# A two-layer decoder: the stores of turned keys and queries take the main part and the rest of one head in one transfer

## The chip, the cores and the metric

The kernel runs on one core of a Trainium2 chip and computes the whole forward pass in one launch. Its engines work side by side, each through its own queue of instructions: TensorE (PE in the profile; PEld is its loading of weights), VectorE (DVE), ScalarE (ACT), GpSimd (POOL) and SyncE (SP). Transfers are issued by SP and by POOL. The metric is the device time of one execution in microseconds.

## The reference

A hybrid decoder trunk in float32: sequence S = 1024, model width 1024, 16 heads of 64 in 4 key/value groups, two layers.

```
layer A:  h = rmsnorm(x);  proj = h @ w_in     # queries, keys and values of three branches, gates
          o = g0 * compressed_attention + g1 * attention_on_top_8_selected_blocks + g2 * window_attention(256)
          x = x + o @ w_out;   x = x + swiglu(rmsnorm(x))
shared:   K, V of three dilation groups from rmsnorm(x) @ kv_w
layer B:  q = rmsnorm(x) @ w_q                 # own queries for each of the three dilation groups
          o = three dilated window attentions ((128,1), (512,4), (2048,16)) merged by their softmax denominators
          x = x + o @ w_out;   x = x + swiglu(rmsnorm(x))
out = rmsnorm(x)
```

A relative-position bias (32 buckets, 16 heads) is added to every attention logit.

## The kernel before

**Numbers in two parts.** Where the kernel needs more than one reduced-precision product gives, it splits a float32 array into a main part H and a rest L (`split`): ACT writes H = source (L179, or L183 with a scale), DVE writes L = source - H (L180 and L184). A product is then three matmuls (`mm3`, L229 to L231). Queries and keys are kept as both parts.

**Layer A's projections.** `proj_T` computes 128 columns of the projection for 512 tokens, turned, so that features lie on partitions: 128 features are two heads of 64. The product lies in one of six PSUM banks named `mm`. `evac_q` and `evac_k` split it into two tiles, `sth` (H) and `stl` (L), of 128 x 512, each with two buffers. `store_heads` (L405) writes them to the DRAM arrays `qS` (per head: 64 rows of H, then 64 rows of L, by 1024 tokens) and `kS` (branch, group, part, 64, 1024), with one DMA for each head b and part z, on POOL's queue: four of 64 x 512 (128 KB) for each eviction. `store_blockind` uses an `sth` buffer too. POOL's queue in this stretch also holds the stores of values (`vS`) and of parts of the output weights (`wS`), and near the end the masks of layer A's attention: `load_bias` has POOL cut a window mask `TW` (affine_select) and a row `C` from each bias tile `T`.

**Layer A's attention** works through units of a group and 128 query tokens. SP loads, from `qS`, `kS`, and others, queries `Q` and `QM`, keys `K` and `KF`, window keys `KW`, values `V` and `VW`, and bias tiles `T` (from `sA`). A unit's window keys are two `KW` tiles (`load_kw`): each takes 64 columns of compressed keys (`kc`, L717) and two DMAs of 64 rows from `kS` (L346 and L347, the upper and the lower half). TensorE multiplies them with the queries at L758, turns the weights at L353 (`pt`) and multiplies with the values at L390.

**Layer B's projections** run as 18 jobs (`project_B`), six for shared keys and values and twelve for queries. For each half a job, `rows_out.done` splits the result into `chunk`, a pair of rows of the array `xr`: a tile of 128 x 2 x 1024 whose first row is H and whose second is L. There are four such chunks, taken in turn. After the second half of the tokens four DMAs on POOL (L1585) write 64 x 1024 (256 KB) each to `qB` or `kBs`. The stores of the last job (`last_stores`) wait by an explicit dependency for a bias load of the attention that follows. POOL's queue there also holds a good part of the sums of the projections' fast matrix multiplication (L1190 to L1208).

**What sets the order.** The program is traced in the order in which it is written; a scheduler then orders the instructions of each engine by a simulated timeline and by the dependencies between tiles. A transfer counts on one of eight completion semaphores for its kind of queue, taken in turn, so each transfer of a queue also waits for the one eight places before it.

## Time and profile before

| | |
|---|---|
| Time, three executions | 2796.76, 2796.29, 2792.22 us; median 2796.29 us |
| The profiled execution | 2793.83 us, of which the span is 2792.1 us; mean granted TensorE clock 0.997 |
| Busy in the span | PE 2738.9 (98%), PEld 2218.9, DVE 2214.7 (79%), ACT 1426.8, POOL 1402.8 us (50%) |
| Transfers | 315.13 MB, of these 62.99 MB in 20464 packets of POOL's queue |
| Stores touched by the change | qS 64 and kS 32 of 128 KB, qB 96 and kBs 24 of 256 KB |

All rows come from one profiled execution. The span runs from the first to the last recorded event. Times in the trace are us from its start; "busy" is the time in which an engine had an instruction at work, and what follows a `<-` in a row is the instruction that ended a wait.

### The profile page before, as it was taken

The page shows a single profiled execution, that of the slowest core. Times are in us where ns is not written, and L with a number is a line of the kernel's source. Part 1 is how long each engine was busy: PE and PEld are TensorE (multiplying, and loading weights), DVE is VectorE, ACT ScalarE, POOL GpSimd, SP SyncE. Part 2 cuts the span into 40 slices and gives each one's busy share as a digit, 9 for nine tenths or more (in the row PEclk, how much of TensorE's full clock was granted, in tenths as well). Part 3 has the DMA queues.
Part 4 walks back from the last instruction along what each step waited for, and adds up shares of the span by engine and source line. Part 5 has one row for each costly group of instructions (what it writes and reads, how often), then busy time and mean ns, then how long its engine had stood idle before and what let it go on. Part 6 is the DMA issues. An engine that isn't in the chain of part 4 may idle for free.

```text
span 2792.1 us, 43025 instructions
## 1 busy us (share of the span) xinstructions
PE 2738.9 (98%) x14494; PEld 2218.9 (79%) x14494; DVE 2214.7 (79%) x4527; ACT 1426.8 (51%) x3171; POOL 1402.8 (50%) x1454
## 2 busy tenths in 40 slices
PE   9999999999999999999999999999999999999997
PEld 8988676776788888888778888777778888888886
DVE  5453888887889899989875677688898888888987
ACT  5531777775644343333454444577756433343434
POOL 3135655552465566565457787110014756655652
PEclk9999999999999999999999999999999999999999
DMA  8669443224122322232224555786341211112112
GB/s 237 218 196 298 133 128 105 68 62 159 35 76 69 83 65 68 62 77 62 84 80 116 167 156 159 242 257 187 114 174 44 74 58 57 49 57 61 54 42 83
DMA packets 292924, 315.13 MB, mean 113 GB/s; under 512 B 50428, under 2 KB 229677, under 8 KB 292704
## 3 DMA queue, kind: packets, MB, share of 16 engines
q1 hardware_dynamic: 272240, 249.40, 30.5%
q0 software_dynamic: 20464, 62.99, 7.4%
q8 instruction: 115, 1.88, 0.3%
q14 instruction: 105, 0.86, 0.1%
HBM read 243.96 MB, written 81.95 MB: 117 GB/s over the span
## 4 chain that ended last, share of the span: by engine, by line
PE 85%; DVE 6%; ACT 2%; issue 2%; DMA 2%; POOL 1%; SPq 1%; POOLq 0%; DVEq 0%; ACTq 0%
PE ux L1161 18%; PE uy L1161 15%; PE dx L993 8%; PE o L390 7%; PE pt L353 6%; PE dr L993 6%; PE dr L1161 4%; PE mm L230 3%; PE mm L229 3%; PE mm L231 3%; PE s L758 1%; DVE pl L954 1%; PE s L846 1%; PE s L1808 1%; PE s L845 1%
## 5 line engine op out<-in xcount | busy, mean ns | idle before, releaser
L954 DVE TENSOR_TENSOR pl<-oT,ph 128x512 fp32r<-128x512 f32 x340 | 340.2, 1018 | 72.3 <-PE dr L993 17.4
L953 ACT ACTIVATE ph<-oT 128x512 fp32r<-128x512 f32 x346 | 211.8, 628 | 215.6 <-PE ux L1161 53.3
L954 DVE TENSOR_TENSOR pl<-oTb,ph 128x512 fp32r<-128x512 f32 x232 | 214.7, 948 | 27.2 <-PE dr L993 17.4
L953 ACT ACTIVATE ph<-oTb 128x512 fp32r<-128x512 f32 x238 | 145.5, 628 | 168.7 <-PE ux L1161 53.4
L353 PE MATMUL pt<-ident,P 128*128 128x128 f32 x1536 | 228.0, 278 | 3.3 <-DVE pT L356 1.9
L742 POOL TENSOR_SCALAR P<-P,sm,gates 128x384 f32<-128x384 f32 (+7 forms) x256 | 183.2, 727 | 79.3 <-DVE sm L740 54.8
L353 PEld LDWEIGHTS pt<-ident,P 128*128 128x128 f32 x1536 | 172.9, 140 | 61.8 <-issue 43.0
L998 DVE TENSOR_TENSOR xrfx<-xrfx,dr 128x512 f32<-128x512 f32 x320 | 204.2, 679 | 17.8 <-PE dr L993 17.7
L1354 POOL TENSOR_TENSOR oT<-oT,gffn 128x512 f32<-128x512 f32 x92 | 118.9, 1303 | 196.0 <-DMA oT<-in_ffn_w_up_dram 127.7
L998 DVE TENSOR_TENSOR xrfx<-xrfx,dx 128x512 f32<-128x512 f32 x320 | 204.5, 678 | 2.2 <-PE dx L993 2.2
L738 ACT ACTIVATE P<-P,m 128x384 f32<-128x384 f32 (+7 forms) x256 | 171.1, 670 | 36.0 <-DVE m L851 14.9
L356 DVE COPY pT<-pt 128x512 f32<-128x512 f32 (+1 forms) x224 | 143.2, 648 | 44.5 <-PE pt L353 39.8
L1354 POOL TENSOR_TENSOR oTb<-oTb,gffn 128x512 f32<-128x512 f32 x92 | 111.8, 1226 | 130.8 <-DMA oTb<-in_ffn_w_up_dram 79.0
L356 ACT COPY pT<-pt 128x512 f32<-128x512 f32 x192 | 110.1, 578 | 103.8 <-PE pt L353 100.8
L390 PE MATMUL o<-pT,V 128*64 128x256 f32 x1200 | 160.7, 391 | 2.3 <-ACT pT L356 1.5
L1770 ACT ACTIVATE P<-P,st 128x384 f32<-128x384 f32 (+2 forms) x256 | 139.6, 548 | 32.3 <-DVE st L1765 30.4
L1765 DVE CUSTOM_DVE_ANT_0 P<-s,T 128x384 f32<-128x384 f32 (+2 forms) x256 | 112.9, 478 | 10.5 <-PE pt L353 3.0
L390 PEld LDWEIGHTS o<-pT,V 128*64 128x64 f32 x1200 | 73.6, 136 | 51.8 <-issue 9.9
L993 PE MATMUL dx<-ph 128*128 128x512 f32 x320 | 107.5, 390 | 0.8 <-ACT ph L953 0.8
L993 PE MATMUL dx<-ph,pl 128*128 128x512 f32 x320 | 107.0, 389 | 0.0
L847 DVE CUSTOM_DVE_ANT_0 P<-s,T 128x128 f32<-128x128 f32 (+3 forms) x192 | 99.5, 550 | 8.1 <-PE s L846 7.8
L230 PE MATMUL mm<-hL,wh 128*128 128x512 f32 (+1 forms) x272 | 102.6, 378 | 0.0
(623 smaller groups left out, 8040.3 us busy)
## 6 DMA issues: line engine op xcount, KB each, us to landing
qB<-xrfx POOLq DMA_DIRECT2D x96, 256.0 KB, 4.5
oT<-in_ffn_w_up_dram SPq DMA_DIRECT2D x92, 256.0 KB, 2.9
oTb<-in_ffn_w_up_dram SPq DMA_DIRECT2D x92, 256.0 KB, 2.9
Q<-qB SPq DMA_DIRECT2D x40, 512.0 KB, 6.9
wd<-in_ffn_w_down_dram SPq DMA_DIRECT2D x60, 256.0 KB, 2.6
oT<-in_b_w_q_dram SPq DMA_DIRECT2D x48, 256.0 KB, 5.6
K<-kBs SPq DMA_DIRECT2D x40, 256.0 KB, 7.5
wraw<-in_a_w_in_dram SPq DMA_DIRECT2D x18, 512.0 KB, 6.9
```

Source lines behind the costliest of these rows:

```text
L230: nc.tensor.matmul(ps, lh, rl, start=False, stop=False, skip_group_check=bool(shared))
L353: prev = nc.tensor.transpose(ps[:, i * 128:(i + 1) * 128], h, ident)
L356: copy(t[:, :w], ps[:, :w])
L390: mm = nc.tensor.matmul(po[64 * e:64 * e + 64, :256], v[e], t, start=first and lo == i == 0, stop=last and hi == nb and i == len(ops) - 1, ...
L738: nc.scalar.activation(P[:, e, :n], P[:, e, :n], AF.Exp, bias=mm[:, e:e + 1], scale=-1.0, accum_out=sm[:, e:e + 1])
L742: nc.gpsimd.tensor_scalar(P[:, e, :n], P[:, e, :n], sm[:, e:e + 1], gate(e), op0=OP.mult, op1=OP.mult)
L953: nc.scalar.activation(h, src, AF.Copy)
L954: self.last = (eng or nc.vector).tensor_sub(l, src, f32(h))
L993: nc.tensor.matmul(banks[t], part(a, t)[u], b[v], start=z == 0 and onX != 2, stop=z == 2, skip_group_check=True)
L998: nc.vector.tensor_add(xs, xs, banks[t])
L1161: mm = nc.tensor.matmul(b, x[:, i * 128:(i + 1) * 128], ys[i], start=first and (z, i) == (0, 0), stop=(z, i) == (2, 3), skip_group_check=True)
L1354: nc.gpsimd.tensor_mul(v, v, gains[:, k:k + 4].unsqueeze(2).to_broadcast([128, 4, 128]))
```

## The change

Both parts go into one tile and one store takes both parts of one head. In layer A, `two_parts` makes one tile `st` of 128 x 2 x 512 with two buffers, in place of `sth` and `stl`, and `store_heads` issues one DMA of 64 x 2 x 512 (256 KB) for each head. In layer B the chunk is already one tile; the four DMAs become two of 64 x 2 x 1024 (512 KB). The addresses in `qS`, `kS`, `qB` and `kBs` and the bytes stay the same. The stores fall from 96 to 48 in layer A and from 120 to 60 in layer B.

```diff
     def store_heads(dst, t, cols):
         for b in range(2):
-            for z in range(2):
-                nc.gpsimd.dma_start(dst(b, z)[:, cols], f32(t[z][b * 64:(b + 1) * 64]))
+            nc.gpsimd.dma_start(dst(b)[:, :, cols], f32(t[b * 64:(b + 1) * 64]))
+
+    def two_parts():
+        t = st.tile([128, 2, 512], F32R, name="st", bufs=2)
+        return t, (t[:, 0, :], t[:, 1, :])
...
         def evac_k(i, ch):
             def f(ps, tk):
-                t = [st.tile([128, 512], F32R, name=n, bufs=2) for n in ("sth", "stl")]
-                split(*t, ps)
-                store_heads(lambda b, z: kS[i, 2 * ch + b, z], t, tk)
+                t, hl = two_parts()
+                split(*hl, ps)
+                store_heads(lambda b: kS[i, 2 * ch + b].rearrange("z d s -> d z s"), t, tk)
...
-                t = st.tile([128, 512], F32R, name="sth", bufs=2)
-                nc.scalar.copy(t[:16], raw)
-                nc.gpsimd.dma_start(bS[:, cols], f32(t[:16]))
+                t = two_parts()[0][:16, 0, :]
+                nc.scalar.copy(t, raw)
+                nc.gpsimd.dma_start(bS[:, cols], f32(t))
...
         def evac_q(ch):
             def f(ps, tk):
-                t = [st.tile([128, 512], F32R, name=n, bufs=2) for n in ("sth", "stl")]
-                split(*t, ps, -DH ** -0.5)
-                store_heads(lambda b, z: qS[2 * ch + b, z * 64:(z + 1) * 64], t, tk)
+                t, hl = two_parts()
+                split(*hl, ps, -DH ** -0.5)
+                store_heads(lambda b: qS[2 * ch + b].rearrange("(z d) s -> d z s", d=DH), t, tk)
...
-                    out[a] = t[:, 0, :].bitcast(F32R), t[:, 1, :].bitcast(F32R)
+                    out[a] = t[:, 0, :].bitcast(F32R), t[:, 1, :].bitcast(F32R), t
...
                     for b in range(2):
-                        for z in range(2):
-                            dst = qB[i, 4 * g + 2 * a + b, z * 64:(z + 1) * 64] if kind == "q" else \
-                                kBs[i, 2 * a + b, z]
-                            store = nc.gpsimd.dma_start(dst, f32(t[z][b * 64:(b + 1) * 64]))
-                            if n == len(jobs) - 1:
-                                last_stores.append(store)
+                        dst = qB[i, 4 * g + 2 * a + b].rearrange("(z d) s -> d z s", d=DH) if kind == "q" else \
+                            kBs[i, 2 * a + b].rearrange("z d s -> d z s")
+                        store = nc.gpsimd.dma_start(dst, t[2][b * 64:(b + 1) * 64])
+                        if n == len(jobs) - 1:
+                            last_stores.append(store)
```

The scheduler orders the changed program anew. The lines below give each engine's order at the places of interest; the numbers behind names tell tiles apart and differ between the two programs, and the changed program's lines lie three further down (two behind `rows_out`).

POOL near the end of layer A's projections, before: mask work for attention stands between the stores of main part and rest.

```order
L689 AFFINE_SELECT TW_2538<-T_2536 128x384
L692 COPY C_2535<-T_2536 128x32
L689 AFFINE_SELECT TW_2545<-T_2543 128x384
L692 COPY C_2535<-T_2543 128x32
L689 AFFINE_SELECT TW_2552<-T_2550 128x384
L692 COPY C_2535<-T_2550 128x32
L409 DMA qS<-sth 64x512 x2
L689 AFFINE_SELECT TW_2559<-T_2557 128x384
L692 COPY C_2535<-T_2557 128x32
L409 DMA qS<-stl 64x512 x2
```

And after:

```order
L408 DMA qS<-st 64x2x512 x6
L692 AFFINE_SELECT TW_2478<-T_2476 128x384
L695 COPY C_2475<-T_2476 128x32
L692 AFFINE_SELECT TW_2485<-T_2483 128x384
L695 COPY C_2475<-T_2483 128x32
L692 AFFINE_SELECT TW_2492<-T_2490 128x384
L695 COPY C_2475<-T_2490 128x32
L692 AFFINE_SELECT TW_2499<-T_2497 128x384
L695 COPY C_2475<-T_2497 128x32
L408 DMA qS<-st 64x2x512 x6
```

The mask work of the four heads is no longer parted by a store.

SP at the start of layer A's attention, before: the two window-key tiles of one unit (3164 and 3165), then the `force` and `QM` loads.

```order
L717 DMA KW_3164<-kc_90 128x64
L346 DMA KW_3164<-kS 64x384
L347 DMA KW_3164<-kS 64x384
L717 DMA KW_3165<-kc_91 128x64
L346 DMA KW_3165<-kS 64x384
L347 DMA KW_3165<-kS 64x384
L923 DMA force<-in_force_dram 128x128
L676 DMA QM_2880<-qS 64x4x512
```

After, the first two loads of the first tile (now 3092) are still ahead of `force` and `QM`; the rest stands behind four bias loads, five loads of keys and values, and four more bias loads, of which the last ones are:

```order
L704 DMA K_2933<-bS 16x1024
L725 DMA V_2938<-vS 128x4x64
L688 DMA T_3064<-sA 128x512
L688 DMA T_3071<-sA 128x512
L688 DMA T_3078<-sA 128x512
L688 DMA T_3085<-sA 128x512
L347 DMA KW_3092<-kS 64x384
L720 DMA KW_3093<-kc_91 128x64
L346 DMA KW_3093<-kS 64x384
L347 DMA KW_3093<-kS 64x384
```

So four loads of window keys moved behind fifteen other loads.

TensorE at the first use of these two tiles, before:

```order
L758 MATMUL s<-KW_3164,Q_2872 128x448
L758 MATMUL s<-KW_3165,Q_2872 128x448
L353 MATMUL pt<-ident,P_3119 128x128 x2
L758 MATMUL s<-KW_3164,Q_2874 128x448
L758 MATMUL s<-KW_3165,Q_2874 128x448
L845 MATMUL s<-K_2580,Q_2519 128x512
L846 MATMUL s<-KF_2586,Q_2519 128x512
```

And after:

```order
L353 MATMUL pt<-ident,P_2838 128x128
L353 MATMUL pt<-ident,P_2872 128x128
L761 MATMUL s<-KW_3092,Q_2800 128x448
L761 MATMUL s<-KW_3092,Q_2802 128x448
L848 MATMUL s<-K_2520,Q_2459 128x512
L849 MATMUL s<-KF_2526,Q_2459 128x512
L848 MATMUL s<-K_2520,Q_2461 128x512
L849 MATMUL s<-KF_2526,Q_2461 128x512
L353 MATMUL pt<-ident,P_2838 128x128
...
L761 MATMUL s<-KW_3093,Q_2800 128x448
L761 MATMUL s<-KW_3093,Q_2802 128x448
```

Both products with the first tile now come first, and those with the second after four products with `K` and `KF` and four transposes (`pt`). Six transposes more than before stand ahead of the first product: the two that stood between the products, and four of another unit's weights.

## The prediction

> **What bounds the kernel now.** I read the page's header and totals first, then the chain that ended last, then a table of stretches, and last the waits at the places that the change touches.
>
> ```profile
> span 2792.1 us, 43025 instructions
> ...
> PE 2738.9 (98%) x14494; PEld 2218.9 (79%) x14494; DVE 2214.7 (79%) x4527; ACT 1426.8 (51%) x3171; POOL 1402.8 (50%) x1454
> ...
> PE 85%; DVE 6%; ACT 2%; issue 2%; DMA 2%; POOL 1%; SPq 1%; POOLq 0%; DVEq 0%; ACTq 0%
> ```
>
> TensorE is busy for 98% of the span and carries 85% of the chain; POOL, which issues the stores, is half idle and has 1% of the chain. A saving on POOL counts only where TensorE is waiting for what comes behind POOL. The stores lie in two places: layer A's projections, in the second and third of the stretches below, and layer B's, mostly in the fourth. The stretches read: start and end, length, busy time of each engine (with instructions), the granted clock, DMA share, GB/s.
>
> ```profile
> 100.00:250.00 150.00, 150.00 (x776) 127.35 (x776) 72.44 (x101) 51.64 (x76) 45.97 (x87) 1.00 0.71 223
> 250.00:300.00 50.00, 47.64 (x236) 37.72 (x236) 23.20 (x131) 25.85 (x100) 32.40 (x70) 1.00 0.82 248
> ...
> 1450.00:1750.00 300.00, 298.25 (x1333) 245.92 (x1332) 206.60 (x206) 144.02 (x233) 231.17 (x252) 1.00 0.52 150
> 1750.00:1800.00 50.00, 48.12 (x295) 39.22 (x293) 27.04 (x62) 25.72 (x58) 4.19 (x8) 1.00 0.72 218
> ```
>
> In layer A's projections TensorE has no idle time at all (150.00 of 150). At the passage into attention it idles 2.36 us of 50, in layer B's projections 1.75 of 300, although POOL is 77% busy there, and 1.88 in the stretch behind them. That is 5.99 us in all: the most that anything near these stores could give.
>
> **The change, part by part.** First the issues. The groups show the number of instructions, their busy time and the mean of one in ns; the list of transfers shows the size and the median time from issue to landing.
>
> ```profile
> L1585 POOL DMA_DIRECT2D qB<-xrfx x96 | 51.0, 537 | 15.0 <-ACT xrfx L183 12.6 <-DMA T<-s 2.2
> ...
> L409 POOL DMA_DIRECT2D qS<-sth x32 | 17.1, 537 | 34.8 <-ACT sth L183 32.7 <-DMA wS<-ob 1.8 <-DMA qS<-stl 0.3
> ...
> L409 POOL DMA_DIRECT2D qS<-stl x32 | 16.9, 531 | 12.4 <-DVE stl L184 8.6 <-DMA wS<-ob 1.5 <-DVE bl L545 1.4
> ...
> L1585 POOL DMA_DIRECT2D kBs<-xrfx x24 | 12.8, 539 | 0.8 <-ACT xrfx L179 0.8
> ...
> L470 POOL DMA_DIRECT2D wS<-ob x16 | 9.0, 564 | 15.1 <-DVE ob L466 8.7 <-DVE ob L468 6.1 <-issue 0.3
> ...
> L409 POOL DMA_DIRECT2D kS<-sth x16 | 8.4, 532 | 23.3 <-ACT sth L179 23.3
> L409 POOL DMA_DIRECT2D kS<-stl x16 | 8.4, 529 | 6.4 <-DVE stl L180 6.3
> ```
>
> The stores are 216 issues: 17.1 + 16.9 + 8.4 + 8.4 + 51.0 + 12.8 = 114.6 us of POOL. After the change there are 108 with twice the bytes each. An issue of 128 KB costs 529 to 537 ns, one of 256 KB 537, one of 512 KB over 128 rows (wS) 564, so I take 0.53 to 0.56 us for a joined one: 108 make 57 to 60 us, and POOL is rid of 54 to 57 us. If a joined issue with its extra dimension cost two old ones, nothing would be freed.
>
> Who waited for these stores? The waits of ACT and DVE in layer A's projections and of TensorE in layer B's (total us, times, longest) say it.
>
> ```profile
> ACT sth L183 <- PE mm L231: 45.9, 11, 4.8
> ```
> ```profile
> DVE stl L184 <- DMA qS<-stl: 9.8, 2, 5.2
> ```
> ```profile
> PE ux L1161 <- ACT d L1210: 0.7, 1, 0.7
> PE dr L1161 <- DVE d L1236: 0.6, 1, 0.6
> ```
>
> In layer A the only ones held up were ACT and DVE when they wanted a store buffer back: DVE 9.8 us in two waits. ACT sits idle up to 4.8 us ahead of an eviction, waiting for TensorE's product, and TensorE has six banks to go on in; so none of it reached TensorE, whose idle time there is 0. In layer B what little TensorE waits is for ACT's and DVE's forming of differences (d), not for a store and not for POOL. So the 54 to 57 us are taken off a queue that nobody waits for. What they can give: in layer A 0; at the passage at most 0.5, since its waits are for DVE; in layer B's projections at most 0.5 of the 1.75. I take 0.6 in all, with 0 and the whole 5.99 as bounds.
>
> The Trainium skill's page "DMA: Bandwidth & Descriptors", section "Anatomy of one DMA — SWDGE (gpsimd) path", gives a transfer about 2.0 us of fixed cost and its bytes at 436 GB/s on top; by it 108 transfers fewer would take an estimated 216 us of fixed cost away, and the sum would go far down if those stood in line. No run so far shows them in line: TensorE's idle time in these stretches is 5.99 us.
>
> Second, the new wait. A row of DVE in layer A's projections shows how long it takes for a rest, and the list of transfers the landing of POOL's stores by size.
>
> ```profile
> 255.08 0.69 DVE L184 SCALAR_TENSOR_TENSOR stl<-mm,sth 128x512 fp32r<-128x512 f32 x1 [4.60 <-DMA qS<-stl]
> ```
> ```profile
> qB<-xrfx POOLq DMA_DIRECT2D x96, 256.0 KB, 4.5
> ...
> wS<-ob POOLq DMA_DIRECT2D x16, 512.0 KB, 5.1
> ```
>
> The main part, written by ACT, could leave while DVE was still forming the rest; the joined store waits for both, and both halves of a buffer come free together. One split on DVE is about 0.7 us, a joined transfer's landing lies by the sizes before between 4.5 and 5.1 us. So a buffer is held about 0.7 us longer at the main part. What is queued behind the waiting store on POOL is the next store and, at the passage, the mask work for attention; behind a late buffer stands ACT's next eviction, with its 4.8 us to spare. The wait that DVE had at the rest's buffer becomes ACT's. Cost 0; without that cover, 5.2 us a time at two places.
>
> Third, what the scheduler moved. Apart from the stores the orders of the engines are nearly the same, save at the start of attention A, where SP loads the window keys (KW, two tiles a unit, each of a kc row and two kS halves). Before, both tiles of one unit stand ahead of the force and QM loads; now the lower half of one tile and all of the other, four loads, stand behind those two, eight bias loads (T) and five of K and V. The lines show when SP issued them before, when TensorE used the keys first, and the landing times of that stretch.
>
> ```profile
> 286.97 0.60 SPq L346 DMA_DIRECT2D KW<-kS  x1
> 287.62 0.59 SPq L347 DMA_DIRECT2D KW<-kS  x1
> ...
> 290.19 0.58 SPq L923 DMA_DIRECT2D force<-in_force_dram  x1
> ...
> 297.54 5.46 SPq L685 DMA_DIRECT2D T<-sA  x4
> 304.05 0.50 SPq L717 DMA_DIRECT2D KW<-kc  x1
> ...
> 306.13 0.54 SPq L717 DMA_DIRECT2D KW<-kc  x1
> ```
> ```profile
> 302.01 0.66 PE L758 MATMUL s<-KW,Q 128*128 128x448 f32 x2
> 302.50 0.38 PE L353 MATMUL pt<-ident,P 128*128 128x128 f32 x2
> ...
> 303.12 0.39 PE L845 MATMUL s<-K,Q 128*128 128x512 f32 x1
> ...
> 304.03 1.04 PE L353 MATMUL pt<-ident,P 128*128 128x128 f32 x8
> 305.00 1.08 PE L390 MATMUL o<-pT,V 128*64 128x256 f32 x8
> ...
> 307.35 0.68 PE L758 MATMUL s<-KW,Q 128*128 128x448 f32 x2 [0.46 <-DVE cm L761]
> ```
> ```profile
> T<-sA SPq DMA_DIRECT2D x8, 256.0 KB, 5.4
> KW<-kS SPq DMA_DIRECT2D x13, 96.0 KB, 3.4
> K<-kS SPq DMA_DIRECT2D x3, 256.0 KB, 9.6
> ```
>
> Over the whole execution the loads of KW landed in:
>
> ```profile
> DMA to landing us min/median/max: 1.7/2.6/8.0
> ```
>
> The keys were issued 12 us ahead of use. Now TensorE's order puts six more transposes ahead of their first use (eight take 0.97 us, 304.03 to 305.00, so 0.7): about 302.74. The second tile comes after two more score products (0.49), four of K (0.91, 303.12 to 304.03) and four transposes (0.49): about 304.63. On SP the four loads leave 287.62 to 290.19 empty, so what stood behind moves 2.57 us ahead, and the late half is issued where SP was free again, at 304.05 - 2.57 = 301.48; with 3.4 us it lands at 304.88. The last of the other three follows 2.08 later (304.05 to 306.13), at 303.56, and lands at 306.96. TensorE would stand 304.88 - 302.74 = 2.14 us, and then be at the second tile at 304.63 + 2.14 = 306.77, 0.19 too early: 2.3 us in all. A K load of that stretch took 9.6 us; if the K loads don't come earlier, because the DMA engines and not SP limit them, the issue stays at 304.05 and the stand is 4.9. If landings are as fast as the shortest KW load, 1.7, the half is there at 303.18 and the second tile at 305.26, which costs 0.6. So 0.6 to 4.9, and I take 2.3, from SP's own rows. Of it I give 0.6 back: the 0.46 at 307.35 and one more wait for DVE of that size vanish when DVE has time to catch up. Net 1.7.
>
> A stand of that length may bring a second price. After 1.56 us of idle time at 2063.08 us, eight matmuls took 0.63 instead of 0.39 and the granted clock fell to half for some 2 us.
>
> ```profile
> 2063.08 0.50 PE L229 MATMUL dr<-ph 128*128 128x512 f32 x1 [1.56 <-DVE o L1859]
> ...
> 2064.03 0.63 PE L229 MATMUL dr<-ph 128*128 128x512 f32 x1
> ```
> ```profile
> 2064.00:2066.00 2.00, 2.00 (x6) 1.58 (x5) 2.00 (x3) 0.00 (x0) 0.76 (x1) 0.50 0.36 131
> ```
>
> Eight times 0.24 is 1.9 us, which I leave out of the sum, as idle time at 2060 came in several pieces, and take into the slow side. The Trainium skill's page "TensorE: Matmul & The Clock Gate", Part 1, lets the clock fall after an idle window of about 3.4 us: by it a stand of 2.3 would cost no clock and one of 4.9 would; the row at 2063 shows a fall after less.
>
> **The sum.** -0.6 (POOL) + 0 (the wait for both parts) + 1.7 (late keys) = +1.1 us. On the profiled execution (2793.83 us, its span 2792.1 and 1.7 around it) that is 2794.9. The median of the three executions is 2796.29, 2.5 above it, so the number to compare with other medians is 2796.29 + 1.1 = 2797.4. The executions themselves lie between 2792.22 and 2796.76, and 0.2% (5.6 us) is about what a measurement of this kernel can tell from no change.
>
> **Rivals.** Faster: the freed POOL time reaches TensorE, because the mask copies on POOL in the passage and the products ahead of layer B's differences come earlier. For it speaks POOL's 77% in layer B's projections; against it that no wait of TensorE there names POOL. Taking all 5.99 us of idle time in these stretches gives 2790.3; only with nearly all of it is the change measurable.
>
> Slower: the late window keys at 302 us. With 4.9 us of standing, 1.9 of lowered clock and nothing given back the time is 2796.29 - 0.6 + 6.8 = 2802.5. It decides when the late half lands after 307.0: the stand is then 4.3, with the clock 6.2, less 0.6 is 5.6. For it speaks the 9.6 us of the K loads and a longest KW landing of 8.0; against it that the scheduler also gave TensorE other work ahead.
>
> Nothing happens at all: the bytes and the rows of memory stay what they were, so the transfers keep the DMA engines as long as before, and the loads still land in time. That gives 2796; it lies within the same bound as my forecast.
>
> **How the numbers follow.** No measurable change, my forecast and the last rival together: 0.73. The faster rival 0.13, since it needs all idle time at once. The slower one 0.14, since its bound lies inside the landing times seen. The range goes from the faster rival's end, 2790, to the slower one's, 2803, and leaves out 1 to 2 in 10 for a mechanism that I don't see, or a set of executions at one edge of the spread.
>
> **What the trace after would show.** 48 and 60 stores at 0.53 to 0.56 us each on POOL, POOL's total near 1347 us; landing of a joined store near that of one before, or 0.5 longer; TensorE without idle time at 100 to 250 us; one or two waits of TensorE, 0.6 to 5 us together, at 302 to 307 us ahead of a score product with KW, its releaser a KW load; ACT now waiting for qS stores where DVE did. I'm wrong if joined stores take much longer to issue or land (then ACT's waits rise over 4.8 us and TensorE idles in layer A), or if the order in attention A moves more than this one stand.

## The result: 0.99% slower, and the time went in layer B's projections

Five executions of the changed kernel took 2820.04 to 2823.45 us, median 2821.61; five of the kernel before, on the same chip, 2789.37 to 2796.76, median 2796.29. The medians are 25.3 us apart; the ratio of the means is 1.0099 (95%: 1.0084 to 1.0113). The forecast was 2797.4 with a range to 2803.

The header, totals and chain by engine of the changed kernel's page:

```profile
span 2819.8 us, 42871 instructions
...
PE 2751.4 (98%) x14494; PEld 2223.7 (79%) x14494; DVE 2221.6 (79%) x4527; ACT 1423.0 (50%) x3171; POOL 1353.4 (48%) x1346
...
PE 78%; DVE 8%; DMA 5%; issue 3%; POOL 3%; ACT 2%; SPq 1%; POOLq 0%; DVEq 0%; ACTq 0%
```

POOL lost 49 us of work, and the program became longer by 28: TensorE's share of the chain fell from 85% to 78%, that of transfers rose from 2% to 5%, that of POOL from 1% to 3%. The same stretches as before (start and end, length, busy time of each engine, granted clock, DMA share, GB/s) say where:

```profile
100.00:250.00 150.00, 150.00 (x773) 127.17 (x773) 72.78 (x101) 51.70 (x76) 31.45 (x55) 1.00 0.70 224
250.00:300.00 50.00, 46.07 (x225) 37.45 (x225) 23.25 (x136) 26.64 (x105) 26.18 (x58) 0.97 0.84 244
1450.00:1750.00 300.00, 283.15 (x1235) 229.20 (x1233) 185.42 (x186) 129.33 (x214) 193.76 (x184) 0.98 0.49 136
1750.00:1800.00 50.00, 47.59 (x207) 38.80 (x208) 31.66 (x35) 21.22 (x34) 21.30 (x22) 1.00 0.62 177
```

Layer A's projections are untouched. In layer B's, TensorE gets through 1235 matmul records in 300 us where it got through 1333: 98 fewer at 0.224 us each (298.25 / 1333) is 22 us of work not done. Idle time explains 15.1 of it (298.25 - 283.15); the granted clock, 0.98 for 1.00, about 6 (2% of 300). Fixed places of the program agree: the kernel is 2.6 us late ahead of layer B's projections (1433.3 for 1430.7 us) and 26.9 late at their end (the last product with T1h 1790.9 for 1764.0). It is 32.6 late at the last write to xr, and 27.7 at the end of the span; where the 5.7 us between the projections and that write go, no run separates. What gives about 4.8 us back at the end is POOL's closing instruction, DRAIN, which is issued behind POOL's last work (before and after; of the three durations in ns, shortest, median and longest, the longest is the one meant):

```profile
L1961 POOLq DRAIN  x3: 46/98/11891, 2779.4 to 2791.8; - x3
```
```profile
L1963 POOLq DRAIN  x3: 46/98/4700, 2812.0 to 2819.6; - x3
```

Before, it ends 10.8 us after the last write to xr, when SP has been done for 4.8; after the change it ends 3.6 us after that write and SP, done at 6.0, is last. Its length goes with the number of transfers that POOL issues in the whole program: 11.9 us with 307 (before), 7.0 with 247 (b_only, b_128 and others below), 4.7 with 199 (after). Three runs are out of line, 2.7 in b_rows2k, 2.4 in b_pair and 2.9 in ab_pair, and why stays open. So the end hides about 4.8 us of loss, and the times below, of kernels with different numbers of stores, differ by this too.

What the engines wait for in layer B's projections, 1450 to 1750 us (total us, times, longest): first POOL before, then POOL, ACT and TensorE after.

```profile
POOL oT L1562 <- DMA oT<-in_b_w_q_dram: 27.6, 11, 5.1
```
```profile
POOL oT L1565 <- DMA oT<-in_b_w_q_dram: 54.6, 14, 9.0
```
```profile
ACT xrfx L183 <- DMA qB<-xrfx: 38.9, 7, 6.4
ACT ph L956 <- POOL oT L1206: 20.0, 6, 6.7
```
```profile
PE dr L1164 <- ACT ph L956: 10.9, 5, 2.7
PE ux L1164 <- ACT d L1213: 2.2, 1, 2.2
```

In the kernel before, ACT's wait for POOL's sums, the second of its two rows here, was shorter:

```profile
ACT ph L953 <- POOL oT L1203: 11.3, 5, 5.6
```

Two things are new after the change. POOL, which multiplies each query weight by its gain, waits for the weight load twice as long as before. And ACT waits 38.9 us for the joined stores themselves (before: 0), because it wants their buffer back. Behind ACT stands `ph`, the operand that TensorE waits for. ACT also waits longer for POOL's sums ahead of `ph`, 20.0 us for 11.3: a second way from POOL to TensorE, which does not go over the buffer. The list of transfers (size, median us to landing) and the groups on POOL show the stores:

```profile
qB<-xrfx POOLq DMA_DIRECT2D x48, 512.0 KB, 6.5
...
oT<-in_b_w_q_dram SPq DMA_DIRECT2D x48, 256.0 KB, 6.4
```
```profile
L1587 POOL DMA_DIRECT2D qB<-xrfx x48 | 29.0, 609 | 14.7 <-DVE xrfx L184 12.0 <-DMA T<-s 2.0 <-issue 0.7
...
L408 POOL DMA_DIRECT2D qS<-st x32 | 19.5, 612 | 63.0 <-DVE st L184 54.1 <-DVE bl L548 8.1 <-DVE dg L791 0.7
...
L408 POOL DMA_DIRECT2D kS<-st x16 | 9.7, 610 | 36.2 <-DVE st L180 36.2
...
L1587 POOL DMA_DIRECT2D kBs<-xrfx x12 | 7.3, 613 | 0.0
```

A joined store lands in 6.5 us (two stores of half the size: 4.5 each) and takes 609 to 613 ns to issue instead of 537.

One turn of the loop, from the timeline of POOL, ACT and TensorE, and from the chain in 1600 to 1650 us:

```profile
1608.59 1.22 POOL L1587 DMA_DIRECT2D qB<-xrfx  x2
1609.84 1.30 POOL L1208 TENSOR_TENSOR oT<-oT 128x512 f32<-128x512 f32 x1
1611.07 1.20 POOL L1587 DMA_DIRECT2D qB<-xrfx  x2
...
1621.55 1.04 POOL L1565 TENSOR_TENSOR oT<-oT,gmix 128x512 f32<-128x512 f32 x1 [6.00 <-DMA oT<-in_b_w_q_dram]
```
```profile
1620.76 1.12 ACT L183 ACTIVATE xrfx<-oT 128x512 fp32r<-128x512 f32 x1 [6.43 <-DMA qB<-xrfx]
...
1622.78 0.62 ACT L956 ACTIVATE ph<-oT 128x512 fp32r<-128x512 f32 x1
```
```profile
1619.91 1.07 PE L1164 MATMUL uy<-T2h,pl 128*128 128x512 f32 x4
1623.45 1.22 PE L1164 MATMUL dr<-B21h,ph 128*128 128x512 f32 x4 [2.47 <-ACT ph L956]
```
```profile
1612.14 9.25 DMA oT<-in_b_w_q_dram
...
1631.42 0.52 POOL qB L1587
1631.95 9.78 DMA qB<-xrfx
...
1641.83 1.21 ACT xrfx L183
```

POOL issues four joined stores within 3 to 4 us; a weight load issued among them (1612.14) takes 9.25 us. ACT's write to the store's buffer begins at 1620.76, after 6.43 us of waiting; the `ph` that stands three places behind it in ACT's order ends at 1623.4, and TensorE has stood 2.47 us. The next burst comes 20.3 us later (1628.88), and its last store (1631.95) again holds ACT until 1641.8. The program explains why the store matters: each query job fills two of the four chunks, so a chunk is wanted back two jobs after it was first opened, soon after its stores have left. A job lasts 19.5 us before and 21.3 after (mean distance of the first issues of the bursts used below). ACT's write needs two things, the store's landing and a sum that DVE forms (`oT`, L1182 before, L1185 after). Their times, worked out from the issues and landings in the trace and counted from the first issue of the burst, over the seven bursts from 1605 us on in each kernel (median and range; b_wait, b_noload and b_128 are told of below):

| | last store of the burst landed, us | DVE's sum ready, us |
|---|---|---|
| before | 11.4 (9.7 to 13.7) | 12.2 (11.2 to 14.2) |
| after | 12.1 (11.5 to 12.8) | 9.1 (8.1 to 14.8) |
| b_wait | 12.2 (10.9 to 14.6) | 11.4 (10.5 to 15.5) |
| b_noload | 10.7 (10.3 to 11.2) | 13.5 (12.9 to 15.1) |
| b_128 | 10.5 (8.8 to 10.6) | 14.9 (12.4 to 15.4) |

In the medians the store was 0.8 us ahead of the sum before, and is 3.0 behind it after. Only 0.7 of the 3.8 is a later landing. The other 3.1 is that the burst starts later against DVE's work. That POOL, which issues it, stands for the weights would do this; but in b_wait, where POOL stands 34.4 us for weights against 27.6 before, the sum is 0.8 nearer too, so not all of the 3.1 need be the weights'. And the small 0.7 hides a slower landing: the last store's issue follows the burst's first by 5.0 us before and by 3.1 after, so from its own issue the last store took 6.4 us before and 9.0 after (medians).

### The profile page after: what moved, and what is told of

The parts are those of the page before. It is cut to its first block, busy times and chain, and to the rows that moved or that the text cites. A ratio compares the mean times of both kernels' runs of the same rounds, so it can differ in the third digit from the quotient of the medians.

```text
span 2819.8 us, 42871 instructions
## 1 busy us (share of the span) xinstructions
PE 2751.4 (98%) x14494; PEld 2223.7 (79%) x14494; DVE 2221.6 (79%) x4527; ACT 1423.0 (50%) x3171; POOL 1353.4 (48%) x1346
## 4 chain that ended last, share of the span: by engine, by line
PE 78%; DVE 8%; DMA 5%; issue 3%; POOL 3%; ACT 2%; SPq 1%; POOLq 0%; DVEq 0%; ACTq 0%
PE ux L1164 16%; PE uy L1164 12%; PE dx L996 7%; PE o L390 7%; PE pt L353 6%; PE dr L996 5%; PE mm L229 3%; PE mm L230 3%; PE mm L231 3%; DVE pl L957 2%; PE dr L1164 2%; DMA qB<-xrfx 2%; PE s L761 1%; PE s L849 1%; PE s L1810 1%
## 5 line engine op out<-in xcount | busy, mean ns | idle before, releaser
L957 DVE TENSOR_TENSOR pl<-oT,ph 128x512 fp32r<-128x512 f32 x340 | 347.6, 1040 | 76.1 <-PE dr L996 17.4
L741 ACT ACTIVATE P<-P,m 128x384 f32<-128x384 f32 (+7 forms) x256 | 170.6, 667 | 34.9 <-DVE m L854 14.9
L1565 POOL TENSOR_TENSOR oT<-oT,gmix 128x512 f32<-128x512 f32 x48 | 63.6, 1329 | 91.2 <-DMA oT<-in_b_w_q_dram 63.2
```

The costliest lines, as they stand in the source:

```text
L741: nc.scalar.activation(P[:, e, :n], P[:, e, :n], AF.Exp, bias=mm[:, e:e + 1], scale=-1.0, accum_out=sm[:, e:e + 1])
L957: self.last = (eng or nc.vector).tensor_sub(l, src, f32(h))
```

## The experiments

Ratios are to the kernel before, on the same chip, with their 95% interval. Idle time of TensorE is 300 minus its busy time in 1450 to 1750 us, 1.75 in the kernel before.

**Which layer.** Layer A alone, the diff's upper half:

```diff
-            for z in range(2):
-                nc.gpsimd.dma_start(dst(b, z)[:, cols], f32(t[z][b * 64:(b + 1) * 64]))
+            nc.gpsimd.dma_start(dst(b)[:, :, cols], f32(t[b * 64:(b + 1) * 64]))
```


> Layer A's stores are joined, layer B's are the four of before. Theory: the time was lost in layer B's projections alone, where ACT waited 48.1 us for qB stores before it could write a buffer again, so this run is at before's 2796 within 0.2% (2791 to 2802), and TensorE is busy for more than 297 us of the 300 in layer B's projections. Rival (the new order at the start of layer A's attention costs it): 2805 or more.

2796.07 us, 1.001 (1.0001 to 1.0019), idle time 1.67. Layer B alone, the lower half:

```diff
-                        for z in range(2):
...
-                            store = nc.gpsimd.dma_start(dst, f32(t[z][b * 64:(b + 1) * 64]))
+                        store = nc.gpsimd.dma_start(dst, t[2][b * 64:(b + 1) * 64])
```


> Layer B's stores are joined, layer A's are the four of before. Theory: all of the loss is here, 2816 to 2824, with ACT waiting 40 us or more for qB stores and TensorE idle 10 us or more in layer B's projections. Rival (the order in layer A): under 2803.

2815.8 us, 1.0076 (1.006 to 1.0092):

```profile
1450.00:1750.00 300.00, 280.73 (x1229) 227.14 (x1228) 187.99 (x187) 129.96 (x214) 197.09 (x185) 0.99 0.49 136
```

The two add up: 2.8 + 22.5 = 25.3 us, each with what its shorter DRAIN gives back already taken off (from the last write to xr to the end of the span it is 11.6 us before, 8.6 in a_only and 7.2 in b_only). Layer B is most of the loss.

**Is it the waiting for both parts?** The kernel before, in which the store of the main part also waits for the rest:

```diff
+                            if z == 0:
+                                tc.add_manual_dep(store.ins, rest_of[0].ins.name, ...)
```


> The kernel before, with one dependency more: each store of a main part in layer B also waits for the rest of the same tile to be written. Transfers stay single, 256 KB each. If the loss comes from waiting for both parts, 2814 or more; if it comes from how long a joined transfer takes to land, no more than 5 us over before (under 2802).

2794.62 us, 1.000 (0.9991 to 1.0009), idle time 1.85. The wait costs nothing. The waits of ACT in 1450 to 1760 us:

```profile
ACT xrfx L183 <- DMA qB<-xrfx: 13.6, 3, 5.4
```

ACT can stand for its buffers 13.6 us in three waits, and none of it reaches TensorE; that much is slack. In this kernel the store lands 0.8 us behind the sum in the medians, and it costs nothing.

**The size of the store.** Both parts joined, but in 256 KB: 32 partitions at a time.

```diff
+                        for h in (0, 32):
+                            store = nc.gpsimd.dma_start(dst[h:h + 32], t[2][b * 64 + h:b * 64 + h + 32])
```


> Layer B's joined stores are cut in two by partitions: 32 x 2 x 1024, four for a tile, 256 KB each, as many as before and each with both parts. If the size of one transfer (512 KB, the wait ends with all of it) makes the loss, it falls to under half (under 2808); if a transfer of few partitions or of two parts writes more slowly, or waiting for both parts is to blame, 2815 or more.

2800.4 us, 1.0023 (1.0013 to 1.0032), idle time 5.75, a store lands in 4.8 us. Two thirds of the loss go (7.1 us of 22.5 are left), not all; in the idle time it is more, 5.75 us for b_only's 19.27, since b_quarter has as many stores as the kernel before and so its long DRAIN (11.9 us). Stores of 256 KB from 32 partitions land about as those from 64 do (4.4 in the same stretch before).

**Which of a job's two buffers.** The joined store in the first (L) or in the second (S) half of each job alone (the edit of the first; the second has `a == 1`):

```diff
-                if r == 1:
+                if r == 1 and a == 0:
...
+                        store = nc.gpsimd.dma_start(dst, t[2][b * 64:(b + 1) * 64])
+                elif r == 1:
```

> Only the first of a job's two buffers (a = 0, the one that is open longest and that ACT waited for) has joined stores, the second keeps four single ones. Theory: most of the loss is here, 2806 to 2820. Rival (bytes in large transfers delay everything, whichever buffer they come from): half the loss, about 2804 here and in the next run alike.

> Only the second of a job's two buffers (a = 1) has joined stores. Nothing waited for that buffer, but its stores stand just ahead of the other's on POOL. Theory: under 2802; rival as in the run before: about 2804.

2804.25 us, 1.0033 (1.0021 to 1.0046), and 2803.16 us, 1.0035 (1.0023 to 1.0048); idle time 10.86 and 10.75. The halves cost the same, and a little less than half of the whole each. My theory that one early buffer alone decides fell.

**Changing when a buffer is wanted back.** Calling L's split later; dealing the four buffers out in another order; a fifth buffer, with and without the joined stores.

```diff
-                done(0, 0, st["d0"])
+                if not late:
+                    done(0, 0, st["d0"])
...
+                if late:
+                    done(0, 0, st["d0"])
```


> Layer B's joined stores as in the changed kernel, layer A's as before. One thing more: the split that opens the first buffer of a job is called some 10 us later, after the job before has closed its own (not for the last job). Transfers, sizes and buffers stay the same. Theory: the loss is ACT standing in its queue until the stores of the buffer that it reuses have landed, so with 10 us more it goes almost wholly: under 2800, and ACT waits under 10 us for qB stores. Rival (joined stores delay the weight loads beside them, which POOL and then TensorE wait for): 2810 or more, POOL still waiting 50 us or more for weight loads.

```diff
-        chunk = Turns([xr[:, k:k + 2, :] for k in (0, 4, 2, 6)])
+        chunk = Turns([xr[:, k:k + 2, :] for k in [0, 4, 2, 6, 0] + [4, 2, 0, 6, 2, 4, 6, 0] * 4])
```


> Layer B's joined stores, with the four buffers dealt out in another order, so that a job's first buffer takes over one that a second buffer held, whose stores land about 2 to 3 us earlier. By the theory the first buffer's wait shrinks by that much, and the loss by half or more (2796 to 2808); the rival (weight loads) leaves 2812 or more.

```diff
+        fifth = oT[:, 2:4, :]
+        chunk = Turns([xr[:, k:k + 2, :] for k in (0, 4, 2, 6, 0)] +
+                      [fifth if k is None else xr[:, k:k + 2, :] for k in (None, 4, 2, 6, 0)] * 4 + ...)
```


> Layer B's joined stores, and from the first query job on a fifth buffer in layer A's idle scratch memory, so that a buffer is written again after five openings (2.5 jobs, some 50 us) and not four (2 jobs, some 40 us). Stores, their sizes and weight loads stay the same. Theory (ACT stands at the head of its queue until the stores of the reused buffer have landed): under 2801. Rival (large stores delay the weight loads and so POOL and TensorE): 2811 or more.

> The kernel before, with its single stores, and the same fifth buffer. TensorE was busy for 298 of 300 us in this stretch, so by either theory no change: 2790 to 2800. It tells what the fifth buffer's own shuffling of the scratch memory costs.

None of the three settles its question. b_late took 2816.45 us, 1.008 (1.0064 to 1.0097), but the scheduler left ACT's row where it was, so the write had not been moved. b_swap took 2838.75, 1.0157 (1.014 to 1.0174): in its order a job's first buffer was last opened five openings ago, but its second only three, so that one is wanted back sooner. The fifth buffer needed scratch that other steps use: by itself it cost 17 us (before_five 2811.31, 1.0062, 1.0047 to 1.0077), and with the joined stores 2840.74 (1.0162, 1.0143 to 1.018). The joining costs 29 us there, no less than without the fifth buffer. ACT still waited for stores:

```profile
ACT xrfx L183 <- DMA qB<-xrfx: 28.9, 5, 6.5
...
ACT oT L183 <- DMA qB<-oT: 9.1, 2, 5.1
```

**Taking the weight loads away.** The query weights of the last ten jobs are not loaded; with joined stores in layer B, and with the stores of before. Both kernels multiply by what the memory still holds.

```diff
-                nc.sync.dma_start(v, w[k * 128:(k + 4) * 128, cc:cc + 128]...)
+                if n < 8:
+                    nc.sync.dma_start(v, w[k * 128:(k + 4) * 128, cc:cc + 128]...)
```


> Layer B's joined stores; the weight loads of the ten last query jobs are left out (they multiply what the memory still holds, so the numbers computed are others). Theory (reuse of the buffers): the loss stays for the most part, 2806 or more, ACT still waiting for qB stores. Rival (weight loads delayed by the stores): no loss, under 2800.

> The kernel before without the same weight loads. By both theories within 4 us of before, since TensorE hardly waited there: 2789 to 2799.

2789.86 us, 0.9984 (0.9974 to 0.9994), and 2791.17, 0.9993 (0.9984 to 1.0003). With joined stores and no loads:

```profile
1450.00:1750.00 300.00, 298.01 (x1333) 246.08 (x1332) 194.98 (x205) 145.51 (x233) 199.37 (x201) 1.00 0.40 112
```

The whole loss is gone, 22.5 us, and ACT no longer waits for a qB store, although a store still lands in 6.2 us (median) and the last one 10.7 us after the start of its burst. The theory that the buffers alone decide expected 2806 or more, and fell. This is the experiment that separates most: stores that land in 6.2 us do no harm by themselves. They need loads beside them.

**How the rows of memory lie.** Joined, 64 partitions, but rows of 2 KB, 256 KB a store; then quarters that alternate between the two halves of the partitions.

```diff
+                        for c in (slice(0, 512), slice(512, 1024)):
+                            store = nc.gpsimd.dma_start(dst[:, :, c], t[2][b * 64:(b + 1) * 64, :, c])
```


> Layer B's joined stores cut in two by tokens: 64 x 2 x 512, 256 KB each, four for a tile, rows of 2 KB in place of 4. If a weight load is slow because its rows of 512 B take turns with store rows of 4 KB, it lands sooner with rows of 2 KB and the time is at or below the quarter-by-partitions run (2796 to 2801, POOL waiting at most 46 us for weight loads). If it is only the number of bytes that one transfer puts ahead of it, the same 2800 as that run. If rows of 2 KB are written more slowly, so that a burst lasts longer, 2806 or more.

```diff
+                    for h in (0, 32):
+                        for b in range(2):
...
+                            store = nc.gpsimd.dma_start(dst[h:h + 32], t[2][b * 64 + h:b * 64 + h + 32])
```


> The quarter-by-partitions stores (32 x 2 x 1024, 256 KB), issued so that they take turns between the lower and the upper 64 partitions. If reading from one half of the partitions at a time is the cause, at or below 2798; if not, 2800 to 2802 as with the other order.

2801.78 us, 1.0028 (1.0018 to 1.0038), and 2799.45, 1.0017 (1.0007 to 1.0027). Shorter rows don't help more than smaller stores do (1.0023); in idle time they help less, 10.21 us for 5.75, which the short DRAIN of b_rows2k (2.7 us) hides in the total. The alternation is within the intervals of the plain quarters, so it settles nothing.

**Half of the partitions, or 512 KB?** A store takes one part of both heads over all 128 partitions, 512 KB. The rows then land at other places of qB and kBs than those from which the attention reads them.

```diff
+                    for z in range(2):
+                        dst = qB[i, 4 * g + 2 * a + z] if kind == "q" else ...
+                        store = nc.gpsimd.dma_start(dst, f32(t[z]))
```


> Layer B's stores in as many and as large transfers as the joined ones (two of 512 KB for a tile), but each takes one part over all 128 partitions in place of both parts over 64. (The rows land at other places of qB and kBs, so the numbers computed are others.) If 512 KB in one transfer is the cause, the loss stays: 2810 or more. If 64 partitions are (a transfer reads from half of the partitions only and so writes more slowly; before, four single ones of both halves were under way together), it goes: under 2800, and the landings within a burst follow each other by 1.5 us or less, where joined ones follow by 2 to 3.

2787.04 us, 0.9977 (0.9967 to 0.9987). The table of stretches, and the list of transfers in 1450 to 1760 us, here and in b_only:

```profile
1450.00:1750.00 300.00, 298.98 (x1338) 247.24 (x1338) 203.97 (x206) 143.98 (x233) 204.55 (x201) 1.00 0.45 151
```
```profile
qB<-xrfx POOLq DMA_DIRECT2D x41, 512.0 KB, 3.2
oT<-in_b_w_q_dram SPq DMA_DIRECT2D x48, 256.0 KB, 3.6
```
```profile
qB<-xrfx POOLq DMA_DIRECT2D x36, 512.0 KB, 6.4
oT<-in_b_w_q_dram SPq DMA_DIRECT2D x48, 256.0 KB, 5.8
```

Over the whole run there are 48 of these stores in both, of as many bytes each; over 128 partitions they land in half the time, the loads beside them in 3.6 us instead of 5.8, and TensorE idles 1.02 us. So 512 KB and the number of stores are not enough for the loss; 512 KB out of 64 partitions are. Two differences remain beside the partitions: the main part may leave before the rest is formed, which spreads a burst over 5 us instead of 3, and a partition holds one row of the transfer and not two that go to places 64 rows apart. Nor is 3.2 us the rule for 128 partitions: the 512 KB stores of wS took 5.1 in the kernel before, amid other transfers. Of the 7.7 us that b_128 is ahead of the kernel before, about 4.8 are its shorter DRAIN. The Trainium skill's page "DMA: Bandwidth & Descriptors", section "Rules for kernel authors", says not to split transfers over the two halves of the partitions, since they go one after the other, but to use one over all 128. This pair of rows agrees with the advice, 6.4 against 3.2 us; but the kernel before splits them as well, in 256 KB, and loses nothing by it.

**Getting that with every row in its place.** First one store for a part of both heads, written to where the attention reads it (the two sides of the transfer then have different forms, 128 x 1024 and 2 x 64 x 1024), in layer B, and in both layers by the same edit in `store_heads`:

```diff
+                        dst = qB[i, h:h + 2, z * 64:(z + 1) * 64] if kind == "q" else kBs[i, 2 * a:2 * a + 2, z]
+                        store = nc.gpsimd.dma_start(dst, f32(t[z]))
```


> Layer B's stores take one part of both heads of a tile in one transfer: 128 partitions, 512 KB, two for a tile, to the right places of qB and kBs. As the 128-partition run: 2785 to 2793, at or below before, store rows of 4 KB taking under 200 ns on average and no wait of ACT for qB stores. If what helped there was that the rows went to one contiguous region, 2797 or more.

> The same in both layers: layer A's stores too take one part of both heads (2 x 64 x 512, 256 KB over 128 partitions). Nothing waited for layer A's stores on TensorE, so within 4 us of the run with layer B alone.

2947.16 us, 1.0546 (1.0532 to 1.0561), and 2999.05, 1.0731 (1.0716 to 1.0745). The page's queue of POOL and its groups, in b_pair:

```profile
q0 software_dynamic: 73264, 63.20, 7.7%
```
```profile
L1584 POOL DMA_DIRECT2D qB<-xrfx x48 | 38.9, 811 | 32.4 <-ACT xrfx L183 26.3 <-DVE xrfx L184 2.2 <-DMA T<-s 2.2
```

73264 packets where there were 20464: a burst of four stores has 3648 packets of four bytes where it had 64, and its stores land 15 to 28 us after its start (the last burst of all: up to 34). The second is 52 us slower than the first, where 4 were expected: with such stores in layer A too, TensorE is busy for 143.91 of the 150 us of layer A's projections and for 36.45 of the 50 behind them.

Then with the arrays themselves laid out by pairs of heads, so that both sides have one form; each load of Q becomes two of 64 rows.

```diff
-    qB = dram.tile([3, H, 128, S], F32, name="qB")
+    qB = dram.tile([3, H // 2, 2, 128, S], F32, name="qB")
...
+                        for z in range(2):
+                            nc.sync.dma_start(f32(Q[hh][z * 64:(z + 1) * 64, lo:hi]), ...)
```


> Layer B's stores as in the 128-partition run (one part of both heads, 512 KB, 128 x 1024 on both sides), with qB and kBs laid out by pairs of heads so that the numbers land where they belong; each load of a query tile by attention B becomes two, of 64 rows each. The stretch of layer B's projections as in that run (TensorE busy for 298.5 us or more of 300, no wait of ACT for qB stores). The 64 further loads on SP cost up to some 5 us in attention B: 2786 to 2796 in all. If contiguous targets were not what differs between the 128-partition run and the two slow pair runs, the stretch would be as slow here as there (2900 or more).

2810.05 us, 1.0057 (1.0044 to 1.0071). Its stretches, and TensorE's waits in 1750 to 1850 us:

```profile
1450.00:1750.00 300.00, 298.72 (x1336) 246.62 (x1336) 208.23 (x206) 143.83 (x233) 202.88 (x200) 1.00 0.45 151
1750.00:1800.00 50.00, 41.96 (x224) 34.20 (x224) 23.25 (x54) 22.77 (x51) 2.13 (x4) 0.93 0.55 169
```
```profile
PE s L1795 <- DMA K<-kBs: 5.3, 2, 5.1
```

The projections are as good as with b_128, which bears out that reading; the loss has moved to the start of layer B's attention, where the loads of K come late and the clock falls to 0.93. On SP's queue they stand behind twice as many loads of Q, each now of 64 rows: the first K load is issued at 1762.92 us, 1759.86 before. Of the versions that leave nothing out and put every row where it is read, none beat the kernel before.

**The waits beside the loss.** The last three rows are the kernels whose buffers are dealt out otherwise. Over these kernels, with ACT's waits for qB stores and POOL's for query weights in 1450 to 1760 us:

| | ACT for qB stores, us | POOL for weights, us (longest) | TensorE idle, us |
|---|---|---|---|
| before | 0 | 27.6 (5.1) | 1.75 |
| b_128 | 0 | 48.5 (5.4) | 1.02 |
| b_wait | 13.6 | 34.4 (4.0) | 1.85 |
| b_rows2k | 21.9 | 34.4 (3.6) | 10.21 |
| b_quarter | 23.2 | 46.0 (5.2) | 5.75 |
| b_cross | 25.6 | 40.5 (5.3) | 5.90 |
| s_joined | 28.9 | 63.8 (6.5) | 10.75 |
| l_joined | 29.4 | 57.5 (6.8) | 10.86 |
| after | 38.9 | 54.6 (9.0) | 16.85 |
| b_only | 46.7 | 50.2 (8.9) | 19.27 |
| before_five | 15.9 | 54.9 (6.3) | 11.39 |
| b_five | 38.0 | 83.1 (9.0) | 27.03 |
| b_swap | 38.6 | 91.9 (9.0) | 27.09 |

POOL's waits do not order these kernels (b_128 has 48.5 us and loses nothing). ACT's waits for its buffers nearly do among the kernels with the old buffers (b_rows2k is out of line), but not with the others: b_swap idles 27.09 us with less of ACT's waits than b_only, and there POOL's are the longest. And the weight loads are needed for ACT to wait at all (b_noload). A reading that fits the kernels with the old buffers: joined stores from 64 partitions delay some of the loads issued among them (of those whose landing the trace has, the median takes 5.6 us before and 5.8 in b_only, but the slowest 7.4 and 9.6), POOL waits for these and issues its next burst later, ACT's turn at the buffer then comes ahead of the landing, and TensorE pays what passes the slack. The need for both, slow stores and loads beside them, is shown (b_128, b_noload). The chain from POOL over the buffer to TensorE is argued from the table of bursts; the runs that should have separated the buffer's part from that of the late weights, which also reach ACT's `ph` through POOL's sums (20.0 us for 11.3), did not (b_late, b_swap, b_five), so how the loss divides between the two ways stays open.

## Why the prediction was wrong

**The step that failed** is the sentence that closes "who waited for these stores": that in layer B nobody waits for a store, so that the time is "taken off a queue that nobody waits for". It was read off the waits of the kernel before, where ACT's row is missing. That showed that the stores were in time, not by how much. The margin could have been computed from the trace, 0.8 us in the median of seven bursts, and I never set anything against it. It is not yet the price: in b_wait the store lands 0.8 behind the sum and TensorE still hides it; behind by 3.0, as after the change, it no longer does. The same sentence rests on TensorE's waits, none of which named POOL; but POOL waited for weights (27.6 us in eleven waits), so a transfer that delays these reaches POOL, and I had costed the stores' effect on the loads beside them at nothing without looking at it.

**Landing, mis-sized.** I took 4.5 to 5.1 us, the upper end from the 512 KB store of wS. That one goes over 128 partitions; the joined store measured 6.5, 1.4 above that end. By itself this costs little (b_noload). The cost is what it does to the loads in the same burst, 9.25 us for the one quoted. What the sum lacked for layer B is 22.5 us (b_only), and about 4 more that the shorter DRAIN hides, a gain that the sum lacked too.

**Issue, mis-sized, without weight.** 0.609 to 0.613 us for 0.53 to 0.56; 65.5 us in all for 57 to 60, so POOL is rid of 49.1 and not 54 to 57. POOL's total, 1353.4, is near the 1347 foretold. For TensorE it was worth nothing, as the step said; what fewer transfers were worth came at the program's end, in POOL's DRAIN (about 4.8 us).

**The wait for both parts: 0, right** (b_wait, 1.000). **Layer A's projections: right.** TensorE idles 0 there, and ACT stood for the stores' buffers, as foretold (its waits in 100 to 310 us):

```profile
ACT st L183 <- DMA qS<-st: 26.0, 5, 8.4
```

The longest, 8.4 us, is past the 4.8 from which the forecast expected TensorE to idle; even that was hidden.

**The late window keys: not in this execution.** In the changed kernel no wait of TensorE for a KW load stands in the trace; its waits at 250 to 310 us are for POOL and DVE:

```profile
PE pt L353 <- POOL P L745: 1.9, 1, 1.9
PE s L761 <- DVE cm L764: 0.9, 1, 0.9
```

The passage still lost 1.57 us (46.07 for 47.64). That this is close to the 1.7 foretold is luck, for the cause is another: POOL's new order puts copies of bias tiles ahead of `P`, and they wait for their loads.

```profile
294.24 0.23 POOL L697 COPY C<-T 128x31 f32<-128x31 f32 x1 [1.84 <-DMA T<-sA]
```

In a_only, whose layer A is the changed one, the wait for POOL is there too (2.0 us), and beside it one for the late keys:

```profile
PE s L761 <- DMA KW<-kS: 1.0, 1, 1.0
```

So the late keys were there, at 1.0 of the 2.3 us foretold; in the changed kernel TensorE came to the product later, 4.9 us after the issue of the late half and not 4.0, and found them landed. Layer A alone cost 2.8 us (0.3 to 5.3 by its interval), with some 2.9 given back by its shorter DRAIN: the sum of +1.1 is near it in number, but not by its terms.

**The rivals.** Faster: refuted, POOL's freed time was of no use to TensorE, though the fewer transfers shorten POOL's DRAIN. Slower by late keys: they are not the loss, 1.0 us in a_only and 0 in the changed kernel. Nothing happens: nearly true for layer A, false for layer B, since "the transfers keep the DMA engines as long as before" did not hold. What the prediction named as its own refutation, joined stores that take much longer to land and raise ACT's waits, is what happened, but in layer B and not in layer A where I had put it. The rule weighed there, the fixed 2.0 us for a transfer from the Trainium skill's page "DMA: Bandwidth & Descriptors", section "Anatomy of one DMA — SWDGE (gpsimd) path", would have taken an estimated 216 us away; no run shows such a saving, and by its formula a store of 512 KB would land in an estimated 3.2 us whatever its partitions. The 128-partition store did (3.2), the 64-partition one did not (6.4).

## What to carry to other kernels

Before stores are joined, compute from the trace when each buffer is written again and how much earlier its last store landed: a wait that is absent says only that the margin is not negative. Count partitions as well as bytes when a transfer's landing is borrowed from another row, and look at what is issued in the same few microseconds on other queues. An issuing engine that is half idle has nothing to sell where nobody waits for it; at the end of the program, which waits for it, fewer transfers of POOL were worth about 4.8 us here.

## What the runs showed of the hardware

512 KB from 64 partitions landed in 6.4 us and from 128 in 3.2, beside the same loads; a row of 4 KB took 244 ns of a DMA engine on average in the one (b_only) and 179 in the other (b_128, both from 1450 to 1760 us). That is not the loads' doing: without them (b_noload) it took 235. A store whose two sides differ in form was cut into 3.6 times the packets of POOL's queue, most of them four bytes, and cost 811 ns to issue, against 553 for one of the same size whose sides agree. POOL's DRAIN at the end took 11.9 us after 307 transfers of POOL's queue and 4.7 after 199, with three kernels out of line. And the granted clock fell after some waits of TensorE of about 2 us (2.47 and 1.98, one in each of the first two stretches), while one of 2.71 us that ended at 1561.12 left it at 1.00:

```profile
1620.00:1640.00 20.00, 17.53 (x70) 13.59 (x69) 14.91 (x14) 8.91 (x14) 10.91 (x10) 0.91 0.52 131
1680.00:1700.00 20.00, 17.41 (x64) 13.27 (x63) 11.14 (x12) 6.39 (x11) 10.65 (x11) 0.83 0.60 160
1560.00:1580.00 20.00, 18.88 (x83) 15.52 (x84) 13.88 (x15) 10.01 (x17) 10.53 (x11) 1.00 0.64 165
```

The Trainium skill's page "TensorE: Matmul & The Clock Gate", Part 1, names an idle window of about 3.4 us for that. The first two rows show it after less.
